# The index and turning chain in steps between the first gate's and the values' products, the second gate's products beside the state space

## The chip, the core and the metric

The kernel runs on one core of one Trainium2 chip. The metric is the device time of one execution in microseconds (us): lower is better. An execution counts from its start to its end on the core. The engines go by the profile's names: PE (TensorE, matrix products), DVE (VectorE), ACT (ScalarE), POOL (GpSimd), and SP, the queue that issues the loads.

## What is computed

Two blocks of two layers each work on x of 256 positions x 1024 channels. The change touches the layers of the first block alone. Cut to what matters, one such layer is:

```python
h = rms_norm(x, norm1_g[l]) * (1.0 + sc1) + sh1
proj = h @ w_in[l]
q, k, v, iq, ik, iw, z, xbc, dt_raw, ga, gm = jnp.split(proj, SPLIT_POINTS, axis=-1)
q = apply_rope(rms_norm(q..., q_norm_g[l]), cos, sin)      # 16 heads of 64
k = apply_rope(rms_norm(k..., k_norm_g[l]), cos, sin)
iq = apply_rope(iq..., cos, sin)                           # 8 index heads of 64
ik = apply_rope(ik..., cos, sin)
# index score of query t for key s <= t: sum_h iw[t,h] * relu(iq[t,h] . ik[s])
# each query keeps its 64 best keys; softmax attention over those
o_attn = dsa_attention(q, k, v, iq, ik, iw, n_keep) @ w_attn_o[l]
xbc = silu(causal_dwconv(xbc, ...));  xs, bm, cm = split(xbc)
y = ssd_scan(xs * dt, a_dt, bm, cm) + xs * d_skip          # state space, 4 groups of 8 heads
y = rms_norm(y * silu(z), ssm_norm_g[l])
o_ssm = y @ w_ssm_o[l]
mixed = (sigmoid(ga) * o_attn + sigmoid(gm) * o_ssm) @ w_out[l]
x = x + g1 * mixed                                         # then a feed-forward part
```

sh1, sc1, g1 and their like come from a small product with `w_ada` ("ada" below). The second block (latent attention, gated linear attention, a diagonal state space and a feed-forward part) is the same in both kernels.

## The kernel before

**Weights.** All weights stream from memory as 639 tiles of 128 x 1024 numbers (512 KB). `weight_plan` lists them in the order in which the products take them, and `make` (line 437) brings one tile: SP loads it into one of five buffers `raw` (line 442), ACT copies it to `whi` (line 445), the part that a product in reduced precision can take, and DVE subtracts that to get the rest, `wlo` (line 446). This pair of steps is called a split. A product of one 128x128 block takes three matmuls: `lin_t` (lines 481 to 483) makes channels x positions, `lin_n` (lines 498 to 500) positions x channels with 512 columns. A tile holds eight blocks, so one product of `lin_t` over all 1024 input channels uses one tile. Splits are made three tiles ahead of their use. The "ada" tiles (`in_ada`, 96 of them) share the five `raw` buffers and are turned by PE at lines 696 and 700, in `ada_part`; `mixed` spreads them between the weight tiles of a part of the plan.

**Order.** Every engine works through its own list, in order. A framework sets the lists ahead of the run, by the order of the program text; loads and splits get a higher priority there. A queue that waits lets nothing behind it pass.

**A layer of the first block** (`block1`, line 822) goes through these parts:

1. The products for dt, index keys and index weights (one narrow tile), for index queries iq, q and k (`lin_n`), with the evictions `evict`, and a short chain for dt.
2. The chain. Index keys `ikd` and index queries `iqr` are rotated by `rope_n` (lines 753 to 767, six DVE operations a call) and turned by PE transposes (`transpose_to`, line 671, copied out by ACT at line 672). Then, for the second and the first half of the queries, PE computes index scores (line 923), ACT takes their relu, DVE adds them up (line 928), and eight rounds of MAX and MATCH_REPLACE (lines 933, 934) take out the 64 best keys and leave a `bias`. Then q and k are rotated with gain tables `tbq`, `tbk` that POOL makes from `rows` (line 750), multiplied by their norm (line 951) and turned again (line 671) to qT and kT.
3. The products of the first gate ga and of the second gate gm: eight tiles each (in layer 1 the first four of ga's come before the layer, `EARLY`), each with one tanh on ACT.
4. B and C of the state space: eight tiles, each with a convolution and silu on DVE and ACT (`conv`, `silu2`, lines 963 and 969), and a small product per group (`cbm`).
5. v: two products of `lin_n`, eight tiles in all.
6. Attention (`attention`, first score at line 778) in steps between the 16 products of x.
7. The state space: for each of 16 pairs of heads decay factors `dd` on DVE and ACT, products with them (line 1079), one product of z (eight blocks), and at some pairs one of `w_attn_o` (`attn_out`, table `ATTN_O`); a norm per group (`ssm_norm`, whose `spread` is line 574 and waits for `rr` of `rsqrt`, line 542).
8. The products of `w_ssm_o` with gm, `w_out`, and the feed-forward part.

`load_rows` (line 740) loads a table into `rows`, which has a single buffer; the load for the second block's first layer stands early in SP's queue, in the middle of layer 0 of the first block.

## Time and profile before

| | |
|---|---|
| three runs | 2380.03, 2381.86, 2384.91 us, median 2381.86 us |
| the profiled execution's own time | 2376.68 us |
| its span | 2374.9 us |
| PE busy | 2225.7 us (94%) |
| PE weight loads busy | 2080.9 us (88%) |
| DVE busy | 1752.4 us (74%) |
| ACT busy | 1324.0 us (56%) |
| POOL busy | 63.0 us (3%) |
| chain that ended last | PE 84%, DVE 11%, DMA 3%, ACT 1%, issue 1% |

The span covers the core's instructions, and the profiled execution's own time is 1.8 us more. A busy share is the sum of the durations over the span; PE's matmuls overlap in the records, so that their starts lie closer than their durations. The chain that ended last is followed back from the last instruction, at each step to what released it. The granted clock (PEclk) is 1.00 for 2.4 GHz and 0.50 for 1.2 GHz; a value between is a mean over a stretch. A row of windows gives the busy times in the order PE, PE's weight loads, DVE, ACT, POOL, each with its instructions (x), then the granted clock, the share of the DMA engines and GB/s. A row of the timeline gives start and length, and in brackets the idle time before it and what ended that.

### The profile page before, as it was taken

What the parts mean: (1) busy time and instruction counts of PE and PEld (TensorE: products, weight loads), DVE (VectorE), ACT (ScalarE), POOL (GpSimd) and SP (SyncE); (2) the same over time, 40 slices, a digit from 0 to 9 for tenths busy, and PEclk for the clock granted to TensorE, in tenths of its full rate; (3) what the DMA queues carried; (4) which work ended last, traced back from release to release, by engine and by line L of the source; (5) the groups of instructions that cost most, each with busy time, mean ns of one, the idle gap of its engine ahead of it and who ended that gap; (6) DMA issues with size and microseconds to landing.
All of it is one profiled execution on the core that took longest, in us unless ns stands there. A gap on an engine that the chain in (4) does not pass through costs nothing.

```text
span 2374.9 us, 46399 instructions
## 1 busy us (share of the span) xinstructions
PE 2225.7 (94%) x18142; PEld 2080.9 (88%) x18142; DVE 1752.4 (74%) x3612; ACT 1324.0 (56%) x2462; POOL 63.0 (3%) x94
## 2 busy tenths in 40 slices
PE   7959998999999969998998999999999999899999
PEld 5848887898998868887898999898999998899999
DVE  4685778858978585788869978867886568668853
ACT  4535666546656534566457655656565456565643
POOL 0000001100000000001100000010000000000000
PEclk8979998999999988999999999999999999999999
DMA  8627443475667526443365566544555547445553
GB/s 292 205 93 253 162 160 125 159 259 170 221 223 254 198 78 229 164 168 134 134 231 162 197 215 208 192 159 140 175 178 183 182 152 224 144 136 176 185 184 125
DMA packets 143466, 429.22 MB, mean 181 GB/s; under 512 B 34864, under 2 KB 40976, under 8 KB 143248
## 3 DMA queue, kind: packets, MB, share of 16 engines
q1 hardware_dynamic: 136496, 422.24, 52.9%
q10 hardware_dynamic: 6752, 4.02, 0.5%
q8 instruction: 143, 2.34, 0.4%
q14 instruction: 75, 0.61, 0.1%
HBM read 413.98 MB, written 12.22 MB: 179 GB/s over the span
## 4 chain that ended last, share of the span: by engine, by line
PE 84%; DVE 11%; DMA 3%; issue 1%; ACT 1%; SPq 0%; ACTq 0%; DVEq 0%
PE pmm L481 21%; PE pmm L482 21%; PE pmm L483 21%; PE pmm L498 3%; PE px L696 3%; PE pmm L500 3%; PE pmm L499 3%; DVE wlo L446 2%; PE px L778 1%; DMA raw<-in_ada 1%; PE px L806 1%; PE px L1079 1%; PE px L700 1%; DVE nv L635 1%; PE px L574 1%
## 5 line engine op out<-in xcount | busy, mean ns | idle before, releaser
L446 DVE TENSOR_TENSOR wlo<-raw,whi 128x1024 fp32r<-128x1024 f32 x639 | 780.4, 1222 | 368.6 <-PE pmm L483 236.9
L445 ACT ACTIVATE whi<-raw 128x1024 fp32r<-128x1024 f32 x639 | 674.6, 1059 | 580.2 <-PE pmm L482 377.6
L481 PE MATMUL pmm<-hh,whi 128*128 128x256 f32 x2464 | 707.9, 288 | 17.6 <-DVE gqk L1520 6.9
L483 PE MATMUL pmm<-hh,wlo 128*128 128x256 f32 x2464 | 704.8, 287 | 2.4 <-DVE wlo L446 2.4
L482 PE MATMUL pmm<-hl,whi 128*128 128x256 f32 x2464 | 705.2, 287 | 0.7 <-DVE hl L525 0.4
L481 PEld LDWEIGHTS pmm<-hh,whi 128*128 128x128 f32 x2464 | 477.3, 194 | 27.9 <-DVE gqk L1520 7.3
L483 PEld LDWEIGHTS pmm<-hh,wlo 128*128 128x128 f32 x2464 | 476.9, 194 | 7.9 <-issue 4.4
L482 PEld LDWEIGHTS pmm<-hl,whi 128*128 128x128 f32 x2464 | 477.6, 194 | 5.3 <-issue 2.8
L481 PE MATMUL pmm<-fh,whi 128*128 128x256 f32 x864 | 244.9, 284 | 0.0
L482 PE MATMUL pmm<-fl,whi 128*128 128x256 f32 x864 | 244.5, 283 | 0.0
L483 PE MATMUL pmm<-fh,wlo 128*128 128x256 f32 x864 | 244.3, 284 | 0.0
L481 PEld LDWEIGHTS pmm<-fh,whi 128*128 128x128 f32 x864 | 165.7, 192 | 0.5
L482 PEld LDWEIGHTS pmm<-fl,whi 128*128 128x128 f32 x864 | 165.8, 192 | 0.2
L483 PEld LDWEIGHTS pmm<-fh,wlo 128*128 128x128 f32 x864 | 165.5, 192 | 0.5 <-issue 0.2
L499 PE MATMUL pmm<-wlo,hh 128*128 128x512 f32 x256 | 101.4, 396 | 0.0
L498 PE MATMUL pmm<-whi,hh 128*128 128x512 f32 x256 | 98.4, 403 | 1.1 <-DVE cvb L963 1.1
L500 PE MATMUL pmm<-whi,hl 128*128 128x512 f32 x256 | 98.8, 394 | 0.0
L696 PE MATMUL px<-raw,cwide 128*32 128x128 f32 x1536 | 76.4, 299 | 5.6 <-DMA raw<-in_ada 5.6
L482 PE MATMUL pmm<-yl,whi 128*128 128x256 f32 x256 | 72.9, 287 | 0.1
L483 PE MATMUL pmm<-yh,wlo 128*128 128x256 f32 x256 | 72.1, 286 | 0.0
L481 PE MATMUL pmm<-yh,whi 128*128 128x256 f32 x256 | 72.0, 286 | 0.0
L696 PEld LDWEIGHTS px<-raw,cwide 128*32 128x32 f32 x1536 | 44.3, 116 | 21.9 <-issue 10.9
(553 smaller groups left out, 4250.8 us busy)
## 6 DMA issues: line engine op xcount, KB each, us to landing
raw<-in_w SPq DMA_DIRECT2D x639, 512.0 KB, 3.7
raw<-in_ada SPq DMA_DIRECT2D x96, 512.0 KB, 4.4
csb<-csd SPq DMA_DIRECT2D x16, 512.0 KB, 5.5
phd<-phases SPq DMA_DIRECT2D x8, 512.0 KB, 3.6
phasel<-phd SPq DMA_DIRECT2D x8, 512.0 KB, 4.6
dpd<-dp SPq DMA_DIRECT2D x4, 512.0 KB, 3.3
gl<-gd SPq DMA_DIRECT2D x32, 64.0 KB, 3.3
bl<-in_s5b SPq DMA_DIRECT2D x4, 512.0 KB, 5.5
```

The lines of the kernel that those rows point to most:

```text
L445: S.activation(hi, raw, AF.Copy)
L446: V.tensor_tensor(lo, raw, hi, OP.subtract)
L481: PE.matmul(ps[:m, :n], wh, src.hi(kt), start=q == 0, stop=False)
L482: PE.matmul(ps[:m, :n], wh, src.lo(kt), start=False, stop=False)
L483: PE.matmul(ps[:m, :n], wl, src.hi(kt), start=False, stop=q == len(kts) - 1)
L498: PE.matmul(ps[t][:, :n], src.hi(kt)[:, ts], w[0], start=start, stop=False)
L499: PE.matmul(ps[t][:, :n], src.hi(kt)[:, ts], w[1], start=False, stop=False)
L500: PE.matmul(ps[t][:, :n], src.lo(kt)[:, ts], w[0], start=False, stop=stop)
L574: PE.matmul(ps[:, col + t * 128:col + (t + 1) * 128], r[:, t:t + 1].to_broadcast([128, 128]), ident, start=True, stop=True)
L635: V.scalar_tensor_tensor(v, xt(j), gcol[:, j:j + 1], self.r, OP.mult, OP.mult)
L696: PE.matmul(pa[32 * j:32 * j + 32, :128], cwide[:, i, :], w[:, i * 128:(i + 1) * 128], start=i < 4, stop=i >= 4, skip_group_check=True)
L700: PE.matmul(pa[:, 128:129], part, half4, start=True, stop=True, skip_group_check=True)
```

## The change

- `weight_plan`: the tiles of v now stand behind ga's and ahead of B's and C's. gm's tiles leave this part; each now stands behind every second z tile of the state space. The ada tiles of `ADA_A` (24 in layer 0, 20 in layer 1) are spread over eight weight tiles fewer.
- The chain (part 2) becomes a generator, `turned`, with a yield between steps; `index_scores` is a generator inside it. Each turning (`turn`) is called one step behind the rotation whose result it turns. The second half's scores now come behind the rotation of q's first half, the first half's behind that of q's second half.
- One step is made after each ga product, three after each half of v, one after each product of B or C, and what is left before the attention.
- gm's products, `gate(gm, ...)`, are made in the state space at the even pairs, behind z's product.

The diff, in which "..." stands for the chain's old text (moved into `turned` as it was):

```diff
--- before.py
+++ after.py
@@ -105,24 +105,25 @@
         a = []
         for c in (C_Q + 512, C_K, C_K + 512):
             a += [("w_in", l, kt * 128, c, 512) for kt in range(8)]
-        for c in (C_GA, C_GM):
-            for j in range(EARLY[l] if c == C_GA else 0, 8):
-                a += _slabs_t("w_in", l, c + j * 128, range(8))
+        for j in range(EARLY[l], 8):
+            a += _slabs_t("w_in", l, C_GA + j * 128, range(8))
+        for c in (C_V, C_V + 512):
+            a += [("w_in", l, kt * 128, c, 512) for kt in range(8)]
         for g in range(4):
             a += _slabs_t("w_in", l, C_XBC + 2048 + g * 128, range(8))
             a += _slabs_t("w_in", l, C_XBC + 2560 + g * 128, range(8))
-        for c in (C_V, C_V + 512):
-            a += [("w_in", l, kt * 128, c, 512) for kt in range(8)]
         plan += mixed(a, ada(l, ADA_A[l]))
         a = []
         for j in range(16):
             a += _slabs_t("w_in", l, C_XBC + j * 128, range(8))
         plan += mixed(a, ada(l, ADA_X[l]))
-        outs = iter(range(8))
+        outs, gms = iter(range(8)), iter(range(8))
         for g in range(5):
             for j in range(4):
                 if g < 4:
                     plan += _slabs_t("w_in", l, C_Z + (4 * g + j) * 128, range(8))
+                    if j % 2 == 0:
+                        plan += _slabs_t("w_in", l, C_GM + next(gms) * 128, range(8))
                 for _ in range(ATTN_O[g][j]):
                     plan += _slabs_t("w_attn_o", l, next(outs) * 128, range(8))
         a = []
@@ -894,23 +895,9 @@
         S.dma_start(csd, dtcs[0:32])
 
 
-        ikd = t256("ikd").rearrange("p (t c) -> p t c", t=2)
...
-        for t in (1, 0):
+        bias, TT = {}, {}
+
+        def index_scores(t, iqT, ikT):
             nk = 128 * (t + 1)
             iws = tiny(8, "iws")
             V.tensor_scalar(iws, mN[:, t, 96:104], IDX_SCALE, None, OP.mult)
@@ -928,6 +915,7 @@
                         V.scalar_tensor_tensor(sc, rl[:, i * nk:(i + 1) * nk],
                                                iws[:, 2 * (j + i) + e:2 * (j + i) + e + 1],
                                                cz if j + e + i == 0 else sc, OP.mult, OP.add)
+            yield
             for r in range(8):
                 m8 = tiny(8, "m8")
                 V.max(m8, sc)
@@ -936,22 +924,51 @@
             V.tensor_tensor(sc, sc, cz, OP.min)
             bias[t] = sc
 
-
-        TT = {}
...
+        def turned():
+            ikd = t256("ikd").rearrange("p (t c) -> p t c", t=2)
+            ikT = t256("ikT")
+            iqT = slot(name="iqT")
             for t in range(2):
+                c_, s_ = rcos[:, t, :], rsin[:, t, :]
+                for r in range(2):
+                    rope_n(ikd[:, t:t + 1, r * 64:(r + 1) * 64], mN[:, t:t + 1, 32:96], c_, s_, c_, s_, 1, 32, V)
+            yield
+            turn = lambda: transpose_to(ikT.rearrange("p (t c) -> p t c", t=2), [ikd[:, t, :] for t in range(2)],
+                                        128, 128)
+            for t in range(2):
+                c_, s_ = rcos[:, t, :], rsin[:, t, :]
+                iqr = t512("iqr")
+                rope_n(iqr.rearrange("p (h d) -> p h d", d=64), iqN[:, t, :].rearrange("p (h d) -> p h d", d=64),
+                       c_, s_, c_, s_, 8, 32, V)
+                turn()
+                yield
+                turn = lambda t=t, iqr=iqr: transpose_to(iqT[:, :, t * 128:(t + 1) * 128],
+                                                         [iqr[:, j * 128:(j + 1) * 128] for j in range(4)], 128, 128)
+            rs = {nm: rsqrt(mean_eps(ss[nm], 32, 64), 32) for nm in "qk"}
+            for nm, gofs in (("q", 0), ("k", 64)):
+                tb = gain_tables(rows, gofs, rcos, rsin, 32, "tb" + nm)
+                TT[nm] = [slot(name=nm + "T"), slot(name=nm + "T")]
+                for t in range(2):
+                    r = rs[nm][:, t * 16:(t + 1) * 16]
+                    xr = slot(name=nm + "r").rearrange("p a b -> p (a b)")
+                    x3 = xr.rearrange("p (h d) -> p h d", d=64)
+                    rope_n(x3, qk[nm][t].rearrange("p (h d) -> p h d", d=64), tb[:, 0, t], tb[:, 1, t],
+                           tb[:, 2, t], tb[:, 3, t], 16, 32, V)
+                    V.tensor_tensor(x3, x3, r[:, :, None].to_broadcast([128, 16, 64]), OP.mult)
+                    turn()
+                    yield
+                    yield
+                    if nm == "q":
+                        yield from index_scores(1 - t, iqT, ikT)
+
+                    def turn(nm=nm, t=t, xr=xr):
+                        for q in range(2):
+                            transpose_to(TT[nm][q][:, :, t * 128:(t + 1) * 128],
+                                         [xr[:, (q * 4 + j) * 128:(q * 4 + j + 1) * 128] for j in range(4)], 128, 128)
+            yield
+            turn()
+
+        side = turned()
         qT = lambda hh: TT["q"][hh // 8][64 * (hh % 2):64 * (hh % 2) + 64, (hh // 2) % 4, :]
         kT = lambda hh: TT["k"][hh // 8][64 * (hh % 2):64 * (hh % 2) + 64, (hh // 2) % 4, :]
 
@@ -968,10 +985,19 @@
             S.activation(th, u, AF.Tanh, scale=0.5)
             V.scalar_tensor_tensor(u, th, 1.0, u, OP.add, OP.mult)
 
-        for gs in (ga, gm):
-            for j in range(EARLY[l] if gs is ga else 0, 8):
-                pg = lin_t("w_in", h, range(8))
-                S.activation(gs[j // 4][:, j % 4, :], pg[:, :T], AF.Tanh, scale=0.5)
+        def gate(gs, j):
+            pg = lin_t("w_in", h, range(8))
+            S.activation(gs[j // 4][:, j % 4, :], pg[:, :T], AF.Tanh, scale=0.5)
+
+        for j in range(EARLY[l], 8):
+            gate(ga, j)
+            next(side, None)
+        vN = [slot(name="vn").rearrange("p a b -> p (a b)") for _ in range(2)]
+        for hf in range(2):
+            for t, p_ in enumerate(lin_n("w_in", h, range(8), 512)):
+                S.activation(vN[t][:, hf * 512:(hf + 1) * 512], p_, AF.Copy)
+            for _ in range(3):
+                next(side, None)
 
         cbms = []
         for g in range(4):
@@ -981,6 +1007,7 @@
                 bc[nm] = t256("cv" + nm)
                 conv(ps[:, :T], "c", 16 + 4 * i + g, 4, bc[nm])
                 silu2(bc[nm])
+                next(side, None)
 
             cbm = t384("cbm")
             pc = px()
@@ -990,11 +1017,8 @@
             S.activation(cbm[:, 128:256], pc[:, 128:256], AF.Copy, scale=0.25)
             V.scalar_tensor_tensor(cbm[:, 256:384], pc[:, 256:384], 0.25, C("tri"), OP.mult, OP.mult)
             cbms.append(cbm)
-        vN = [slot(name="vn").rearrange("p a b -> p (a b)") for _ in range(2)]
-        for hf in range(2):
-            for t, p_ in enumerate(lin_n("w_in", h, range(8), 512)):
-                S.activation(vN[t][:, hf * 512:(hf + 1) * 512], p_, AF.Copy)
-
+        for _ in side:
+            pass
         o = new_hl(8, "o")
 
         ys = [None] * 4
@@ -1089,6 +1113,8 @@
                 S.activation(zz, pz[:, :T], AF.Tanh, scale=0.5)
                 V.scalar_tensor_tensor(zz, zz, 1.0, pz[:, :T], OP.add, OP.mult)
                 V.tensor_tensor(xs[:, pair, :], xs[:, pair, :], zz, OP.mult)
+                if pair % 2 == 0:
+                    gate(gm, 2 * g + pair // 2)
                 attn_out(ATTN_O[g][pair])
                 if pair in NORM_AT and g:
                     if pair == NORM_AT[0]:
```

Three places of the order, before and now. Helper lines are one higher in the changed kernel (446 is 447, 671 is 672, 740 is 741), 923 is 910, 933 and 934 are 921 and 922, 951 is 957, 963 is 980, 969 is 986.

PE, layer 0, from the last product of k to the first tile behind the chain, before (`px` and `pmm` are accumulators, `cst` holds the identity, `raw,cwide` and `half,adap` are ada):

```order
L483 MATMUL pmm<-hh,wlo 128x256
L671 MATMUL px<-cst_75,iqr 128x128 x8
L923 MATMUL px<-ikT,iqT 128x256 x8
L923 MATMUL px<-ikT,iqT 128x128 x8
L671 MATMUL px<-cst_75,qr 128x128 x16
L671 MATMUL px<-cst_75,kr 128x128 x13
L696 MATMUL px<-raw,cwide 32x128 x16
L671 MATMUL px<-cst_75,kr 128x128 x3
```

The same engine and layer in the changed kernel, at the second half's scores (line 910) and q's first turning (line 672):

```order
L499 MATMUL pmm<-whi,hh 128x512
L910 MATMUL px<-ikT,iqT 128x256 x2
L500 MATMUL pmm<-wlo,hh 128x512
L501 MATMUL pmm<-whi,hl 128x512
L499 MATMUL pmm<-whi,hh 128x512
L500 MATMUL pmm<-wlo,hh 128x512
L672 MATMUL px<-cst_75,qr 128x128 x6
L697 MATMUL px<-raw,cwide 32x128 x8
L672 MATMUL px<-cst_75,qr 128x128 x2
```

The turnings and scores of the chain stood in a row on PE; now products of v (lines 499 to 501) stand between them.

DVE, layer 1, at B's and C's convolutions. Before, the chain had ended there and splits and convolutions took turns:

```order
L934 MATCH_REPLACE bias<-m_9877,bias 128x128
L935 TENSOR_SCALAR bias<-bias 128x128
L936 TENSOR_TENSOR bias<-bias,cst_76 128x128
L446 TENSOR_TENSOR wlo<-raw,whi 128x1024 x6
L963 SCALAR_TENSOR_TENSOR cvb<-pmm,pp_78,cvb 128x255
L963 SCALAR_TENSOR_TENSOR cvb<-pmm,pp_78,cvb 128x254
L963 SCALAR_TENSOR_TENSOR cvb<-pmm,pp_78,cvb 128x253
L446 TENSOR_TENSOR wlo<-raw,whi 128x1024
```

Now, between two splits (the first and the last row here are instructions 1236 and 1247; the split before is 1231):

```order
L980 SCALAR_TENSOR_TENSOR cvc<-pmm,pp_78,cvc 128x253
L766 TENSOR_TENSOR ru<-kn,tbk 128x512
L767 TENSOR_TENSOR rv<-kn,tbk 128x512
L922 MATCH_REPLACE bias<-m_10156,bias 128x256
L986 SCALAR_TENSOR_TENSOR cvb<-th,cvb 128x256
L986 SCALAR_TENSOR_TENSOR cvc<-th,cvc 128x256
L768 TENSOR_TENSOR kr<-ru,rv 128x16x32
L921 MAX m_10159<-bias 128x8
L957 TENSOR_TENSOR kr<-kr,rr 128x1024
L922 MATCH_REPLACE bias<-m_10159,bias 128x256
L921 MAX m_10162<-bias 128x8
L447 TENSOR_TENSOR wlo<-raw,whi 128x1024
```

Rotations of k and rounds of the choice of keys now stand among the convolutions: 15 instructions between these two splits, 18 between the second of them and the next.

SP's queue, layer 0, around the load of `rows`, before:

```order
L442 DMA raw<-in_w 128x1024
L692 DMA raw<-in_ada 128x1024
L740 DMA rows<-in_rows 128x192
L442 DMA raw<-in_w 128x1024 x2
L692 DMA raw<-in_ada 128x1024
```

Now:

```order
L693 DMA raw<-in_ada 128x1024
L443 DMA raw<-in_w 128x1024
L741 DMA rows<-in_rows 128x192
L693 DMA raw<-in_ada 128x1024
L443 DMA raw<-in_w 128x1024
```

Before, the load of `rows` stood ahead of the weight tile of gm's first product; now it stands ahead of a tile of the third group's B and C, 13 weight tiles further on.

## Rows read from the trace of the kernel before

**Rows 1.** Waits of PE, whole run: us in total, times, longest.

```profile
PE px L671 <- DVE qr L951: 27.2, 4, 8.8
PE px L574 <- DVE rr L542: 24.5, 7, 7.5
PE px L671 <- DVE kr L951: 19.6, 4, 5.6
```

**Rows 2.** Windows: stretch, us, each engine's busy time, PEclk, DMA share, GB/s.

```profile
102.30:258.60 156.30, 130.47 (x1128) 115.63 (x1126) 106.57 (x235) 68.52 (x138) 4.32 (x8) 0.90 0.53 177
127.50:164.50 37.00, 12.65 (x85) 10.58 (x89) 33.10 (x75) 8.65 (x17) 4.32 (x8) 0.60 0.02 3
832.60:975.40 142.80, 118.81 (x960) 104.19 (x958) 100.54 (x230) 61.06 (x120) 5.24 (x8) 0.86 0.49 164
863.80:895.00 31.20, 8.02 (x47) 6.42 (x46) 30.67 (x69) 5.29 (x13) 5.24 (x8) 0.58 0.00 1
895.00:900.00 5.00, 5.00 (x56) 3.37 (x55) 4.26 (x20) 2.15 (x5) 0.00 (x0) 0.50 0.56 189
900.00:905.00 5.00, 5.00 (x52) 3.48 (x52) 2.66 (x8) 2.58 (x8) 0.00 (x0) 0.50 0.78 252
```

**Rows 3.** Timeline of PE in layer 0: start, us, operation, idle before.

```profile
126.85 1.30 PE L671 MATMUL px<-cst,iqr 128*128 128x128 f32 x8 [0.28 <-DVE iqr L767]
128.84 3.99 PE L923 MATMUL px<-ikT,iqT 64*128 64x256 f32 x32 [0.69 <-ACT iqT L672]
141.63 1.94 PE L671 MATMUL px<-cst,qr 128*128 128x128 f32 x8 [8.80 <-DVE qr L951]
```

**Rows 4.** Timeline of PE at products and one ada column behind it.

```profile
172.01 0.28 PE L481 MATMUL pmm<-hh,whi 128*128 128x256 f32 x1
172.13 0.28 PE L482 MATMUL pmm<-hl,whi 128*128 128x256 f32 x1
...
172.97 0.28 PE L700 MATMUL px<-half,adap 128*128 128x1 f32 x2
...
173.75 0.38 PE L483 MATMUL pmm<-hh,wlo 128*128 128x256 f32 x1
```

**Rows 5.** Waits of SP's queue, 120 to 170 us.

```profile
SPq L740 <- POOL tbk L750: 37.3, 1, 37.3
```

**Rows 6.** Timeline of SP's queue, 120 to 170 us.

```profile
123.38 0.33 SPq L692 DMA_DIRECT2D raw<-in_ada  x1
...
164.66 1.18 SPq L442 DMA_DIRECT2D raw<-in_w  x2
```

**Rows 7.** Groups of DVE, 108 to 300 us: busy us, mean ns, idle.

```profile
L446 DVE TENSOR_TENSOR wlo<-raw,whi 128x1024 fp32r<-128x1024 f32 x42 | 51.3, 1222 | 40.1 <-PE pmm L483 17.7 <-ACT whi L445 12.6 <-PE pmm L499 7.9
...
L933 DVE MAX8 m<-bias 128x8 f32<-128x256 f32 x8 | 3.4, 420 | 0.1
L934 DVE MATCH_REPLACE8 bias<-m,bias 128x256 f32<-128x256 f32 x8 | 3.2, 406 | 0.0
...
L951 DVE TENSOR_TENSOR qr<-qr,rr 128x1024 f32<-128x1024 f32 x2 | 2.4, 1210 | 0.0
...
L963 DVE SCALAR_TENSOR_TENSOR cvc<-pmm,pp,cvc 128x253 f32<-128x253 f32 x4 | 1.9, 478 | 0.1
...
L761 DVE TENSOR_TENSOR ru<-kn,tbk 128x512 f32<-128x512 f32 x2 | 1.5, 740 | 0.0
...
L765 DVE TENSOR_TENSOR ru<-kn,tbk 128x512 f32<-128x512 f32 x2 | 1.4, 680 | 0.0
```

**Rows 8.** Windows of the state space, layers 0 and 1.

```profile
346.60:446.00 99.40, 89.07 (x691) 78.17 (x690) 82.47 (x197) 57.42 (x119) 16.96 (x13) 0.93 0.39 129
1061.70:1161.60 99.90, 87.18 (x690) 77.14 (x689) 83.95 (x206) 59.10 (x127) 18.60 (x20) 0.95 0.37 130
```

**Rows 9.** Waits of PE in the state space of layer 0, from 372 us.

```profile
PE px L574 <- DVE rr L542: 7.5, 1, 7.5
```

**Rows 10.** Waits of PE in the state space of layer 1, from 1088 us.

```profile
PE px L574 <- DVE rr L542: 10.6, 2, 7.5
```

More of the change, by code (lines that the diff above doesn't have):

```diff
@@ L894, in block1 @@
         S.dma_start(csd, dtcs[0:32])
-        ikd = t256("ikd").rearrange("p (t c) -> p t c", t=2)
-        ikT = t256("ikT")
-        iqT = slot(name="iqT")
-        for t in range(2):
-            c_, s_ = rcos[:, t, :], rsin[:, t, :]
-            for r in range(2):
-                rope_n(ikd[:, t:t + 1, r * 64:(r + 1) * 64], mN[:, t:t + 1, 32:96], c_, s_, c_, s_, 1, 32, V)
-        transpose_to(ikT.rearrange("p (t c) -> p t c", t=2), [ikd[:, t, :] for t in range(2)], 128, 128)
-        for t in range(2):
-            c_, s_ = rcos[:, t, :], rsin[:, t, :]
-            iqr = t512("iqr")
-            rope_n(iqr.rearrange("p (h d) -> p h d", d=64), iqN[:, t, :].rearrange("p (h d) -> p h d", d=64),
-                   c_, s_, c_, s_, 8, 32, V)
-            transpose_to(iqT[:, :, t * 128:(t + 1) * 128], [iqr[:, j * 128:(j + 1) * 128] for j in range(4)],
-                         128, 128)
-        bias = {}
-        for t in (1, 0):
+        bias, TT = {}, {}
+        def index_scores(t, iqT, ikT):
             nk = 128 * (t + 1)
@@ L937, in block1 @@
             bias[t] = sc
-        TT = {}
-        rs = {nm: rsqrt(mean_eps(ss[nm], 32, 64), 32) for nm in "qk"}
-        for nm, gofs in (("q", 0), ("k", 64)):
-            tb = gain_tables(rows, gofs, rcos, rsin, 32, "tb" + nm)
-            TT[nm] = [slot(name=nm + "T"), slot(name=nm + "T")]
-            for t in range(2):
-                r = rs[nm][:, t * 16:(t + 1) * 16]
-                xr = slot(name=nm + "r").rearrange("p a b -> p (a b)")
-                x3 = xr.rearrange("p (h d) -> p h d", d=64)
-                rope_n(x3, qk[nm][t].rearrange("p (h d) -> p h d", d=64), tb[:, 0, t], tb[:, 1, t],
-                       tb[:, 2, t], tb[:, 3, t], 16, 32, V)
-                V.tensor_tensor(x3, x3, r[:, :, None].to_broadcast([128, 16, 64]), OP.mult)
-                for q in range(2):
-                    transpose_to(TT[nm][q][:, :, t * 128:(t + 1) * 128],
-                                 [xr[:, (q * 4 + j) * 128:(q * 4 + j + 1) * 128] for j in range(4)], 128, 128)
+        def turned():
+            ikd = t256("ikd").rearrange("p (t c) -> p t c", t=2)
+            ikT = t256("ikT")
+            iqT = slot(name="iqT")
+            for t in range(2):
+                c_, s_ = rcos[:, t, :], rsin[:, t, :]
[35 more added lines that the diff above has]
+            turn()
```

## The prediction

> **What bounds the kernel now.** I read the waits of PE first, since PE is busy 94% of the span and heads the chain that ended last. Of its waits for DVE the largest are those of the turnings: 27.2 us for qr and 19.6 for kr, four each, and between them 24.5 for the norms' rr [rows 1]. All eight waits for qr and kr lie in two stretches, one per layer. In layer 0's stretch of 37.0 us PE is busy 12.65 and DVE 33.10; in layer 1's of 31.2 us PE 8.02 and DVE 30.67 [rows 2]. So the chain is DVE's, and PE waits for each of its steps, up to 8.80 us before one turning [rows 3]. DMA stands at 0.02 and 0.00 there [rows 2]: no raw buffer comes free. PE runs at the lower clock level for much of it (mean 0.60 and 0.58), and in layer 1 products go on at 0.50 for ten us behind the hole [rows 2]. The stage around each hole, from k's last product to the first attention score, takes 156.3 and 142.8 us [rows 2].
>
> **The change, part by part.**
>
> *The holes.* In the new order products of ga, v, B and C stand between the chain's steps, so PE has work while DVE rotates. What is won is the hole less PE's own work in it, which moves along. In layer 0 that work is 12.65 us of busy time at a mean clock of 0.60; all of it halved would be 7.6. Group by group: the last iqr turnings 0.65 and 32 of q and k at 1.94 per eight, both halved for the full clock (0.65 and 3.9), the scores 4.0 as they stand [rows 3], one ada column 1.0 (from 172.97 to 0.23 us behind 173.75) [rows 4]: 9.5. Won: 37.0 − 9.5 = 27.5. In layer 1 the same reading makes 5.4 of the 8.02: 25.8, and about 6 more for the products that run at 0.50 behind the hole, ten us certain and some two beyond. Won: 31.8. Together 59.3.
>
> *gm.* Eight products leave each stage and join the state space: 64 blocks of three matmuls 0.12 us apart [rows 4] are 23.0 us of PE, and eight splits on DVE at 1.222 [rows 7] 9.8. ACT moves with them and has 42 us idle in the state space of layer 0 (57.42 of 99.40) [rows 8]. By itself the move is worth nothing: 23.0 off one place and 23.0 on the other, if PE sets both.
>
> *Does PE set the shorter stage?* Layer 0: 156.3 − 27.5 − 23.0 = 105.8 us for PE, against DVE's 106.57 − 9.8 = 96.8 [rows 2, 7]. It fits, if no split comes late. Layer 1: 142.8 − 31.8 − 23.0 = 88.0, against DVE's 100.54 − 9.8 = 90.7. There DVE is the longer by three us even if it never idles. That is where a new wait must appear: PE for wlo, or for cvb and cvc.
>
> *The new waits.* DVE takes its list in order, so a split stands behind whatever the chain put ahead of it. In layer 1 the order shows 15 instructions between two splits: four conv steps at 0.48, six of the rotation at 0.68 to 0.74 or 1.21 for the multiplication by rr, five of MAX and MATCH_REPLACE at 0.42 and 0.41, two of silu near 0.42 [rows 7]; with the split they come to about 8.5 us less their small overlaps, and the next period to about 8.1. A tile gives PE 24 matmuls at 0.12, 2.9 us, with an ada column 3.9. Three tiles are split ahead, so one such period is covered (8.5 against 3 times 2.9 to 3.9) and two in a row are not: 17 against 12 leave some 5 us, and with the three us above I take 9 for layer 1. In layer 0 the chain is spread over 24 products and DVE has 9 us to spare: 4 for turnings that come while DVE is still at qr or kr. Bounds for both layers together: none at all, and one us on each of the 16 tiles of v, B and C per layer, 32.
>
> *Loads.* The load of rows now blocks SP. Before, it waited 37.3 us for POOL's tbk [rows 5], and no raw tile was issued between 123.38 and 164.66 us [rows 6]. tbk's new version needs its buffer, which DVE's last rotation of k frees. In the new order that load stands 13 weight tiles later, near the time at which the rotation ends. Five raw buffers cover some 7.8 us (two tiles of 3.9) of a block. Between nothing and ten us, I take 2. The bytes themselves fit: about 44 tiles of 0.524 MB in 105 us are 220 GB/s; the queue reached 252 from 900 to 905 us, while PE never paused [rows 2].
>
> *The state space.* PE is busy 89.07 of 99.40 and 87.18 of 99.90 us [rows 8], so 10.3 and 12.7 us are idle there. Most of it is one or two waits at the norm's spread for rr: 7.5 and 10.6 [rows 9, 10]. Where 30 product matmuls stood between a norm's first matmuls and its spread, 163 stand now: 133 more at 0.12 are 16 us of cover. On the other side DVE goes from 82.47 to 92.3 us there, and its splits stand ahead of rr's eleven small steps. Between none and all 23.0 of this idle time is filled; I take 5 a layer, 10.
>
> **Sum.** −59.3 + 4 + 9 + 2 − 10 = −54.3. The profiled execution's own time is 2376.7; that gives 2322.4. The median of the three runs is 5.2 above it, so **2327 us** for the median of the changed kernel. Of the 54 us some 44 come from the stages and 10 from the state space.
>
> **Two rules weighed.** What the order shows for DVE, that a split never passes the rotation ahead of it, is the first place where the sum may be too kind. The Trainium skill, "TensorE: Matmul & The Clock Gate", section "Architectural detail: the array is 16× 32×32, not 1× 128×128", says that ScalarE and VectorE take their queues strictly first in, first out; by that rule each of the chain's pieces delays the split behind it, as in rival A.
> The second is the clock. In the holes the long idle times go with a mean clock of 0.60 and 0.58 [rows 2], and in the state space many short ones with 0.93 and 0.95 [rows 8]. The new stages will have short ones. The same page, section "A second HAM failure mode: psum-queue depth-cycling", says that frequent small idle times between groups of matmuls can make the clock swing between its levels; by that rule rival B holds.
>
> **Rivals.**
>
> A. *The splits queue behind the chain.* One us of wait on each of 32 tiles in place of my 13 in all, so 19 more: **2346**. For it: DVE is 91% and more of the shorter stages (96.8 of 105.8; 90.7 of 88.0). Against it: splits are made three tiles ahead, and the periods of 8 us are few.
>
> B. *The clock swings.* If the stages run at the state space's mean of 0.94, their 194 us of PE work (105.8 + 88.0) lose 6%, 12 us: **2339**. Against it: outside the hole layer 0's stage had (0.90 × 156.3 − 0.60 × 37.0) / 119.3 = 0.99 [rows 2].
>
> C. *All of it is filled.* No new waits, and all 23.0 us of the state space: 15 + 13 less, **2299**. For it: DVE has room in layer 0 and the cover of the norms is twice their wait. Against it: layer 1, where DVE is longer than PE.
>
> D. *DVE becomes the bound through both stages.* PE then waits in the v, B and C tiles for the chain's whole time, 33.1 + 30.7 = 63.8 us, with the 2 of the rows load, and nothing is filled in the state space: −59.3 + 63.8 + 2 = +6.5, so **2388**, slower. It decides from a mean wait of 59.3 less 2 over 32 tiles, 1.8 us a tile; at that point the change is worth nothing, 2382. Against it: outside the holes DVE now idles 119.3 − 73.5 = 45.8 us in layer 0's stage and 111.6 − 69.9 = 41.7 in layer 1's [rows 2], time that the chain's 33.1 and 30.7 us can take.
>
> That the change doesn't do what it says is out: the order shows the chain's matmuls among products, and gm's behind z.
>
> **The numbers.** My forecast 0.52, A 0.20, B 0.10, C 0.10, D 0.04, and 0.04 for D at its turning point, no gain. Faster 0.92, same 0.04, slower 0.04; a measurement of this kernel tells about 0.2%, 4.8 us, from no change. The range leaves out D and most of C: it reaches from 2302, my own terms at their lower bounds (waits of 2, the state space's idle time filled to all but a few us), to 2352, A with little of the state space filled (2346 and 6).
>
> **What would show it.** Right: the waits of PE for qr and kr fall from 46.8 to under 10; no stretch of 30 us with PE under half busy and DMA near zero; first attention score of layer 0 about 110 us behind k's last product, of layer 1 about 97; the half clock behind the hole gone; gm's matmuls in the state space, which takes 117 us (99.4 + 23.0 − 5) with less wait for rr. A would show as PE waiting for wlo at v, B and C, some 30 us; B as a granted clock under 0.96 in the stages; the load of rows as one more gap in SP's raw loads of over 10 us; D as stages of 130 us and more. My sum is wrong if the state space grows by over 25 us, or if the stages lose less than 30 us each beyond gm's 23.

## The result and the profile after

The changed kernel takes 2315.93 us (median of four runs, 2314.76 to 2319.71), the kernel before in the same job 2382.2 us (four runs, 2380.03 to 2384.91). The ratio is 0.9728, with a 95% interval of 0.9711 to 0.9745: 2.7% faster. The forecast was 2327, with a range of 2302 to 2352.

The profiled execution takes 2316.91 us by its own time, with a span of 2315.1, against 2376.68 and 2374.9 before: 59.8 less, where the sum said 54.3. The medians lie 66 apart, since the profiled execution of before was 5 below its median and this one 1 above.

The page's first part, engines over the whole run:

```profile
PE 2214.8 (96%) x18142; PEld 2077.9 (90%) x18142; DVE 1745.4 (75%) x3612; ACT 1319.7 (57%) x2462; POOL 64.8 (3%) x94
```

PE's share rises from 94 to 96%; the work is the same, in a shorter span. The chain that ended last is 88% PE and 7% DVE now, 84 and 11 before. PE's waits over the whole run (columns as in [rows 1]):

```profile
PE pmm L482 <- DVE xs L980: 11.4, 4, 2.9
PE px L799 <- DVE sc L792: 9.5, 3, 4.6
PE pmm L482 <- DVE cvb L980: 9.3, 4, 4.9
PE pmm L482 <- DVE gqk L1546: 7.3, 2, 4.1
PE px L575 <- DVE rr L543: 6.4, 4, 2.1
```

The waits for qr (27.2) and kr (19.6) of [rows 1] are gone, and rr's 24.5 has become 6.4, none of it over 2.1. In their place stand waits for xs and cvb: PE wants an accumulator that a convolution on DVE has not read out yet.

By stage, as windows (columns as in [rows 2]): from k's last product to the first attention score, from there to the first product of w_attn_o, and from there to the first of w_ssm_o, layer 0 and then layer 1:

```profile
103.05:217.20 114.15, 111.09 (x997) 98.33 (x995) 99.52 (x234) 60.98 (x126) 5.69 (x8) 0.99 0.64 218
217.20:306.70 89.50, 82.32 (x603) 74.16 (x603) 73.81 (x176) 57.27 (x144) 0.00 (x0) 0.94 0.41 138
306.70:411.60 104.90, 102.07 (x829) 91.86 (x828) 86.23 (x192) 64.53 (x129) 13.33 (x12) 1.00 0.45 146
798.35:903.30 104.95, 96.67 (x843) 85.90 (x841) 92.72 (x226) 54.09 (x110) 7.57 (x8) 0.98 0.60 200
903.30:991.20 87.90, 80.04 (x588) 71.96 (x588) 73.23 (x177) 56.87 (x145) 0.00 (x0) 0.94 0.40 136
991.20:1096.10 104.90, 102.07 (x828) 91.87 (x827) 86.38 (x189) 63.88 (x128) 17.74 (x19) 1.00 0.43 144
```

The first and fourth answer to the stages of [rows 2], the third and sixth to [rows 8]. The second and fifth, attention beside x's products, were before:

```profile
258.60:346.60 88.00, 83.45 (x629) 73.80 (x629) 76.30 (x175) 60.06 (x147) 0.00 (x0) 1.00 0.44 144
975.40:1061.70 86.30, 83.72 (x629) 73.70 (x629) 74.59 (x166) 58.19 (x139) 0.00 (x0) 1.00 0.43 146
```

PE is busy for 111.09 of 114.15 us where the hole of layer 0 was, at a clock of 0.99 (0.90 before). In layer 1 it is busy 96.67 of 104.95 and DVE 92.72. The state space runs at 1.00 with PE busy 102.07 of 104.90. What has become worse is attention beside x: 0.94 for 1.00, and 7.2 us idle in place of 4.6 in layer 0 and 7.9 in place of 2.6 in layer 1.

| | layer 0 | layer 1 |
|---|---|---|
| k's last product to the first attention score | 156.30 to 114.15 | 142.80 to 104.95 |
| to the first product of w_attn_o | 88.00 to 89.50 | 86.30 to 87.90 |
| to the first product of w_ssm_o | 99.40 to 104.90 | 99.90 to 104.90 |

The first two lines together lose 40.65 and 36.25 us, the third gains 5.5 and 5.0. The rest of the span is 6.6 longer, 3.5 of it right behind the state spaces (up to the first product of w_up), the remainder in parts that the change leaves alone. PE's waits in the first stage of layer 0, then of layer 1, then in layer 0's state space; behind them SP's for the load of rows in layer 0's first stage:

```profile
PE pmm L482 <- DVE cvb L980: 2.4, 2, 2.0
PE px L701 <- ACT adap L700: 0.7, 2, 0.4
```

```profile
PE pmm L482 <- DVE cvb L980: 6.9, 2, 4.9
PE px L701 <- ACT adap L700: 0.7, 1, 0.7
PE pmm L482 <- DVE cvc L980: 0.4, 1, 0.4
```

```profile
PE px L1103 <- DVE xdtn L1057: 1.5, 2, 1.0
PE pmm L482 <- ACT gm L990: 1.3, 1, 1.3
```

```profile
SPq L741 <- POOL tbk L751: 3.6, 1, 3.6
```

That load waits 3.6 us where it waited 37.3 [rows 5], and PE waits for no weight there.

### The profile page after: what moved, and what is told of

It reads as the page before. It is cut to its first block, busy times and chain, and to the rows that moved or that the text cites. A ratio compares the mean times of both kernels' runs of the same rounds, so it can differ in the third digit from the quotient of the medians.

```text
span 2315.1 us, 46342 instructions
## 1 busy us (share of the span) xinstructions
PE 2214.8 (96%) x18142; PEld 2077.9 (90%) x18142; DVE 1745.4 (75%) x3612; ACT 1319.7 (57%) x2462; POOL 64.8 (3%) x94
## 4 chain that ended last, share of the span: by engine, by line
PE 88%; DVE 7%; DMA 3%; ACT 2%; issue 1%; SPq 0%; ACTq 0%; DVEq 0%
PE pmm L482 22%; PE pmm L483 22%; PE pmm L484 22%; PE pmm L499 3%; PE pmm L500 3%; PE pmm L501 3%; PE px L697 2%; DVE wlo L447 2%; DMA raw<-in_w 1%; PE px L779 1%; PE px L807 1%; PE px L1103 1%; ACT whi L446 1%; PE px L672 1%; DMA raw<-in_ada 1%
## 5 line engine op out<-in xcount | busy, mean ns | idle before, releaser
L482 PE MATMUL pmm<-hh,whi 128*128 128x256 f32 x2464 | 712.0, 290 | 38.2 <-DVE xs L980 11.4
L482 PEld LDWEIGHTS pmm<-hh,whi 128*128 128x128 f32 x2464 | 482.4, 196 | 47.1 <-issue 11.3
L484 PEld LDWEIGHTS pmm<-hh,wlo 128*128 128x128 f32 x2464 | 482.1, 196 | 6.2 <-issue 2.9
L483 PEld LDWEIGHTS pmm<-hl,whi 128*128 128x128 f32 x2464 | 482.7, 196 | 4.8 <-issue 2.1
L697 PE MATMUL px<-raw,cwide 128*32 128x128 f32 x1536 | 66.5, 287 | 4.3 <-DMA raw<-in_ada 4.0
```

Of the source, the lines that this page charges most:

```text
L482: PE.matmul(ps[:m, :n], wh, src.hi(kt), start=q == 0, stop=False)
L483: PE.matmul(ps[:m, :n], wh, src.lo(kt), start=False, stop=False)
L484: PE.matmul(ps[:m, :n], wl, src.hi(kt), start=False, stop=q == len(kts) - 1)
L697: PE.matmul(pa[32 * j:32 * j + 32, :128], cwide[:, i, :], w[:, i * 128:(i + 1) * 128], start=i < 4, stop=i >= 4, skip_group_check=True)
```

## Experiments

Times are medians, ratios those to the kernel before on the same chip, which took 2378.61 us beside the steps alone, gm's move alone, v's place alone and gm in the last group; 2377.88 beside gm's and v's move together, turning at once, half of gm in layer 1's first stage and the chain through before B and C; and 2378.87 beside the last three.

**The steps without gm's move.** gm's products and tiles go back behind ga's; nothing else differs from the change.

```diff
+        for j in range(8):
+            gate(gm, j)
...
-                if pair % 2 == 0:
-                    gate(gm, 2 * g + pair // 2)
```

> The chain in steps as in the change, v ahead of B and C, but gm's eight products back in their old stage, behind ga's. Theory: the two parts of the change add up. The state space then falls back to its old waits (99.4 and 99.9 us from the first product of w_attn_o to the first of w_ssm_o, waits for rr of 7 us and more, granted clock about 0.94), which cost 12 us a layer; layer 1's stage gains up to 7 us back, since gm's products give DVE time: 2316 + 24 - 7 to 0, so 2333 to 2340. Rival: gm's move is worth nothing by itself (the state space is shorter for another reason): 2316, within 5.

2333.95 us, 0.9809 (0.9794 to 0.9823): 44.7 less than before. The state space of layer 0 is the old one; layer 1's is 4.3 us shorter than it was (windows of both, PE's waits in layer 0):

```profile
324.77:424.32 99.55, 89.24 (x690) 78.33 (x689) 81.76 (x196) 57.39 (x119) 16.50 (x13) 0.93 0.36 126
1021.05:1116.58 95.53, 87.08 (x690) 76.48 (x689) 82.29 (x193) 57.57 (x119) 20.06 (x21) 0.98 0.38 132
```

```profile
PE px L575 <- DVE rr L543: 7.4, 1, 7.4
PE px L1105 <- DVE xdtn L1059: 2.9, 2, 2.2
```

In layer 1 PE waits 5.4 us for rr there, in two waits, where it waited 10.6 [rows 10]: the theory had its old 99.9 us and did not see this. So the steps are worth 44.7 us and gm's move, on top of them, 18 (2333.95 to 2315.93). The two stretches ahead of the state space are 17.4 and 17.2 us longer than in the change, which is what the six gm products take that the change moves out of them (6 x 2.88 = 17.3): layer 1 won nothing by having gm's products there.

**gm's move without the steps.** The kernel before with gm's tiles and products moved as in the change; the chain stays in one piece and v behind B and C.

```diff
-        for gs in (ga, gm):
-            for j in range(EARLY[l] if gs is ga else 0, 8):
-                pg = lin_t("w_in", h, range(8))
+        for j in range(EARLY[l], 8):
+            gate(ga, j)
...
+                if pair % 2 == 0:
+                    gate(gm, 2 * g + pair // 2)
```

> The kernel before with gm's products moved into the state space and nothing else: the chain in one piece, v behind B and C. Theory: the holes of 37 and 31 us stay as they were (waits for qr and kr 47 us), and the state space with gm takes 105 us instead of 99.4 + 17.3, with no wait for rr above 1 us: 2382 - 24 = 2358, from 2354 to 2362. Rival: the state space was shorter only because the stage ahead of it handed it over differently: 2382, within 5.

2373.63 us, 0.9983 (0.9971 to 0.9995): five us, not 24. The state space did what was expected (104.90, as in the change). The time went elsewhere: in layer 0 the two stretches ahead of it should have lost 17.3 us and lost 1.2, in layer 1 they lost 12.6. (The profiled execution took 2378.93 us, 5.3 above this kernel's median, so that a part of the loss read here may be this execution's own.) Windows of this kernel behind the hole and of its state space, its waits of PE for the ada tiles between 100 and 250 us, then windows of the kernel before at the first two of these times:

```profile
165.00:180.00 15.00, 11.04 (x129) 8.27 (x122) 3.88 (x4) 5.52 (x16) 0.00 (x0) 0.89 0.84 299
180.00:200.00 20.00, 18.32 (x148) 16.39 (x147) 7.08 (x10) 8.02 (x19) 0.00 (x0) 0.74 0.58 204
346.00:450.90 104.90, 102.07 (x828) 91.87 (x827) 86.23 (x192) 64.49 (x129) 13.32 (x12) 1.00 0.43 145
```

```profile
PE px L697 <- DMA raw<-in_ada: 3.5, 3, 1.7
PE px L701 <- ACT adap L700: 1.9, 2, 1.0
```

```profile
165.00:180.00 15.00, 14.19 (x175) 11.94 (x163) 9.20 (x25) 7.72 (x20) 0.00 (x0) 0.98 0.91 336
180.00:200.00 20.00, 20.00 (x209) 17.51 (x209) 7.24 (x6) 10.65 (x23) 0.00 (x0) 1.00 0.84 287
```

Before, PE left the hole at nearly full clock and worked without a pause. Without gm's products there it idles 4.0 and 1.7 us in the first two windows, in short waits for ada tiles, and the granted clock falls to 0.74: a clock 0.26 lower for 20 us is at most 5.2 us of work.

**v's move added to that.** The kernel of the last run, with v's tiles and products ahead of B's and C's.

```diff
+        vN = [slot(name="vn").rearrange("p a b -> p (a b)") for _ in range(2)]
...
         cbms = []
...
-        vN = [slot(name="vn").rearrange("p a b -> p (a b)") for _ in range(2)]
```

> gm's products moved into the state space and v's ahead of B and C, as in the change, but the chain in one piece. It differs from the run with gm alone by the place of v. Theory: with gm alone moved the stage of layer 0 lost 13 us, since B and C with their convolutions and the ada columns then followed right behind the hole, where gm's plain products had stood; v's plain products there give it back, and the state space keeps its 12 us a layer: 2374 - 10 = 2364, from 2360 to 2367. Rival: the loss is the loads' and the clock's, which any product behind the hole meets: 2374, within 4.

2364.67 us, 0.9937 (0.9922 to 0.9952), within the theory's range. Behind the hole:

```profile
165.00:180.00 15.00, 12.39 (x145) 10.10 (x143) 5.67 (x8) 7.62 (x19) 0.00 (x0) 1.00 0.90 308
180.00:200.00 20.00, 20.00 (x129) 15.49 (x130) 7.88 (x7) 9.69 (x16) 0.00 (x0) 1.00 0.74 262
```

With v's products in that place the clock is 1.00 and PE is busy throughout from 180 to 200 us. So behind a hole it matters what follows; and gm's move is worth 13 us without the steps, if v's goes with it. The steps (44.7) and these two moves (13.2) add up to 57.9, and the change gives 66.3, or 63.8 when it was run again.

**v's place alone.** The change with v, and its six steps of the chain, behind B and C.

```diff
-        vN = [slot(name="vn").rearrange("p a b -> p (a b)") for _ in range(2)]
...
+        vN = [slot(name="vn").rearrange("p a b -> p (a b)") for _ in range(2)]
...
         for _ in side:
             pass
```

> The change, with v's products (and the three steps behind each half of v) behind B and C again. Theory: the chain's steps then stand among B's and C's products, each of which brings about 4 us of convolution and silu to DVE, so that PE waits longer for accumulators that cvb and cvc hold: 8 us in layer 1 become 15 to 20, 3 us in layer 0 become 8 to 10, while DVE idles in v's: 2328 to 2336. Rival: where v stands is worth nothing, since the list of DVE is the same in sum: 2316, within 5.

2313.02 us, 0.9719 (0.9702 to 0.9735): no different from the change. The theory fell. With no hole left, v's place is worth nothing: waits of 7.8 us in layer 0's stage, in place of 3.1, but 7.2 in layer 1's, in place of 8.2. The theory's 4 us of DVE work per product of B or C was too much: three convolution steps of 0.48 us and a silu of 0.42 are 1.9.

**Turning at once.** The change delays each turning by a step. Here it is made in the step of its rotation.

```diff
-                    turn()
+                    for q in range(2):
+                        transpose_to(TT[nm][q][:, :, t * 128:(t + 1) * 128],
+                                     [xr[:, (q * 4 + j) * 128:(q * 4 + j + 1) * 128] for j in range(4)], 128, 128)
                     yield
                     yield
```

> The change, with each turning made in the step of its own rotation instead of one step later. Theory: the order of PE's list is set by when operands are reckoned to be ready, so that products still stand between a rotation and its turning, and the delay of a step is worth nothing: 2316, within 4, waits for qr and kr under 5 us in all. Rival: the delay is what lets products cover the rotations; without it PE waits for qr and kr again, 2 to 4 us at each of eight turnings: 2332 to 2348.

2333.91 us, 0.9809 (0.9795 to 0.9824): 18 us lost, as the rival had it in sum, though not by eight waits. Layer 0's stage as windows and its largest waits, then layer 1's largest wait:

```profile
104.20:170.00 65.80, 65.10 (x534) 56.17 (x532) 51.38 (x120) 30.04 (x61) 5.78 (x4) 1.00 0.60 207
170.00:200.00 30.00, 21.47 (x192) 18.57 (x192) 24.39 (x60) 11.53 (x26) 1.35 (x4) 0.79 0.54 164
200.00:231.60 31.60, 29.60 (x280) 27.94 (x278) 24.96 (x54) 17.84 (x39) 0.00 (x0) 0.93 0.64 218
```

```profile
PE pmm L482 <- DVE cvb L977: 4.0, 3, 2.0
PE px L672 <- DVE kr L958: 3.0, 1, 3.0
PE pmm L482 <- ACT whi L446: 2.4, 1, 2.4
```

```profile
PE px L672 <- DVE kr L958: 7.2, 1, 7.2
```

Until 170 us nothing is lost. Then k's rotations come, among B and C. In 30 us PE is idle for 8.5, where the change idles 3.1 in the whole stage, and the clock stands at 0.79, which is at most 6.3 us of work. In the change neither stage has a wait for kr: the delay of a step keeps k's turnings out of PE's way.

**All of gm's products in the last group.** The change with two gm products behind each z of group 3.

```diff
-                if pair % 2 == 0:
-                    gate(gm, 2 * g + pair // 2)
+                for j in range(2 if g == 3 else 0):
+                    gate(gm, 2 * pair + j)
```

> The change, with all eight of gm's products in the last group of the state space, two behind each z, instead of spread over the groups. The state space does the same work. Theory: gm's products gain time as cover for the norms of the first groups; 70 products of 0.12 us now stand ahead of the first norm's spread in place of 172 (30 in the kernel before), so a wait for rr of 3 us comes back there, with some time at the lower clock level: 2316 + 3 to 8 a layer, 2322 to 2332. Rival: any more work on PE there gains the same: 2316, within 4.

2327.2 us, 0.9781 (0.9767 to 0.9796): 11 lost, within the theory's range, though its wait of 3 us came back as one of 7.5 in layer 0 and one of 4.4 in layer 1. In layer 0's state space:

```profile
300.65:421.93 121.28, 113.18 (x890) 102.38 (x889) 94.26 (x214) 69.33 (x139) 14.39 (x13) 0.93 0.41 136
```

```profile
PE px L575 <- DVE rr L543: 7.5, 1, 7.5
PE px L1103 <- DVE xdtn L1057: 0.6, 1, 0.6
```

The old wait of 7.5 [rows 9] is back, and the old clock of 0.93 [rows 8]. It is gm's products as cover for the first norm, not more work in general, that the state space wins by.

**Half of gm in layer 1's first stage**, each with a step of the chain, the other four at the first pair of each group.

```diff
+GM_A = (0, 4)
...
+        for j in range(GM_A[l]):
+            gate(gm, j)
+            next(side, None)
```

> The change, with four of gm's eight products of layer 1 back in its first stage, each with a step of the chain; the other four at the first pair of each group of the state space, which leaves 156 products ahead of the first norm's spread. The same work is done. Theory: layer 1's stage waits for DVE (8 us for cvb, cvc and ada), since it is short of PE work beside the chain; 11.5 us more of it take half of that or more away, and the state space stays without a wait for rr: 2308 to 2313. Rival: these waits come from single late convolutions and not from DVE's sum, so they stay: 2316, within 3; or the state space loses its cover again: 2320 to 2326.

2314.55 us, 0.9727 (0.9711 to 0.9743): no different. The waits in layer 1's first stage fell as the theory had it, from 8.2 to 3.8; the state space, at a clock of 0.94 in place of 1.00, lost that again. PE's waits in the stage, then in the state space of layer 1:

```profile
PE pmm L485 <- DVE cvb L983: 3.8, 2, 2.1
```

```profile
PE px L1109 <- DVE xdtn L1063: 3.4, 2, 2.2
PE px L578 <- DVE rr L546: 2.1, 1, 2.1
```

**The chain through before B and C.** Six steps behind each half of v in place of three.

```diff
-            for _ in range(3):
+            for _ in range(6):
                 next(side, None)
```

> The change, with six steps of the chain behind each half of v instead of three, so that the chain is through before B and C. Theory: the sum of DVE's work in the stage decides, not its place; the waits for cvb and cvc (2 and 7 us) go, and about as much comes as waits for turnings among v's products: 2316, within 5. Rival: the rival of the prediction, splits that queue behind the chain: with the chain denser, waits for wlo and for turnings of one us on each of v's tiles and more: 2326 to 2336.

2315.5 us, 0.9731 (0.9716 to 0.9745): no different, as the theory had it. In layer 1's first stage:

```profile
PE px L672 <- DVE kr L957: 4.3, 1, 4.3
PE pmm L482 <- DVE cvb L980: 3.7, 2, 2.2
```

6.9 us of waits for cvb became 3.7, and 4.3 for a turning came: what one order saves, the other takes.

**The waits that are left.** The change again, and two ways to spread attention's 24 steps over x's 16 products.

```diff
-            for _ in range(24 * (n + LAG) // 16 - 24 * (n + LAG - 1) // 16 if n + LAG else 0):
+            for _ in range([1, 1, 1, 1, 1, 1, 1, 1, 1, 1, 1, 1, 1, 1, 1, 1][n]):
                 next(att, None)
```

(In the third run the list holds no step for the first four products and two for each of the others.)

> The changed kernel itself once more, to set the others beside it on one chip: 2316, within 4.

> The change, with one attention step per product of x instead of the old three for every two products; the eight left over follow the last product. Theory: the largest waits that the change has left are two of 2.9 us per layer among x's products, each with some five us at the lower clock level behind it: four products fill the four accumulators while ACT stands at the attention's copies, and their convolutions start together. In the order this happens once per layer with one step a product, and twice now. A gain of 2.9 and some 2.5 us per layer, less what the eight steps cost behind x: 2305 to 2312. Rival: attention's chain of steps takes its time wherever it stands, and what is won among x's products comes back behind them: 2316, within 4.

> The change, with no attention step before the fifth product of x and two per product from there. Theory: in the order there is still one place per layer where four convolutions start together, and two where two or three do, so it gains less than the run with one step a product: 2310 to 2316. Rival: DVE gets time at the start of x to end the chain, and that is what counts: 2303 to 2309.

2315.03 (0.9735, 0.9722 to 0.9748), 2317.5 (0.9753, 0.9732 to 0.9774) and 2311.83 (0.9723, 0.9710 to 0.9736): three times the same within the intervals. The second run's theory fell; the third run lies in its theory's range, but so does the change run again. With one step a product, from the first attention score of layer 0 through its state space (in an execution of 2327.72 us, 10 above that kernel's median):

```profile
PE px L1103 <- DVE xdtn L1057: 3.6, 2, 2.2
PE pmm L482 <- DVE zs L1114: 3.3, 1, 3.3
PE pmm L482 <- DVE xs L980: 2.9, 1, 2.9
PE pmm L482 <- ACT gm L990: 2.6, 2, 1.3
```

One wait of 2.9 for xs went, and one of 3.3 for zs came, in the state space, where the eight steps left over now stand. No kernel tried here is faster than the change by more than the measurement tells.

## Why the prediction was right

The forecast lies 11 us above the measurement. 5.5 of that is the sum (54.3 where the profiles have 59.8), the rest is where the profiled executions stand beside their medians. The mechanism held, but one term of the sum was less than half of what came, and two agreements are in part luck.

**The holes: right in the sum, in part by luck.** The forecast had 59.3 us won and 15 given back as new waits, 44.3 in all. The steps alone gave 44.7. But in that run's profile the stretches up to w_attn_o lost 23.4 and 19.0 us, 42.4 together, with new waits of 2.3 and 4.8; 4.3 more came in layer 1's state space, which this part of the sum did not contain. No run parts what the holes gave from what the new waits took.

**The new waits: right in size, by another path.** Forecast 4 us in layer 0, for turnings that come while DVE is still at qr or kr, and 9 in layer 1, 5 of them for late splits; the stages have 3.1 and 8.2, and none of it is a wait for qr, kr or wlo. It was the other place that the prediction named, cvb and cvc: convolutions of B and C on DVE have yet to read PE's accumulators, and PE waits for one of those. So the two sizes agree by luck. The longest such wait, 4.9 us in layer 1, ended at 867.02 us. DVE's list around it:

```profile
862.73 0.48 DVE L980 SCALAR_TENSOR_TENSOR cvb<-pmm,pp,cvb 128x254 f32<-128x254 f32 x1
864.04 1.22 DVE L447 TENSOR_TENSOR wlo<-raw,whi 128x1024 fp32r<-128x1024 f32 x1 [0.83 <-ACT whi L446]
...
865.57 0.68 DVE L764 TENSOR_TENSOR kr<-ru,rv 128x512 f32<-128x512 f32 x1
...
866.51 0.46 DVE L980 SCALAR_TENSOR_TENSOR cvb<-pmm,pp,cvb 128x253 f32<-128x253 f32 x1
```

Between the last two steps of one convolution stand a split, which itself waited 0.83 us for ACT, and pieces of the chain. So it is DVE's order that holds PE here, as in rival A, but the convolution queues behind the split and the chain, and not the split behind the chain. The prediction's list of the 15 instructions between two splits adds up to 17; they are three convolution steps, five of the rotation, five of the choice of keys and two of silu. The two periods took 8.4 and 7.0 us, where it said 8.5 and 8.1 (splits at 864.04, 872.46 and 879.47 us).

Rival A, splits that queue behind the chain, gave 2346; in the change PE waits 4.1 us at that matmul for wlo in the whole run, 3.7 before. The denser chain, done before B and C, cost nothing either, against rival A's 2326 to 2336 for that run. That DVE sets layer 1's stage was half right: four gm products more there took 4.4 us of waits away, and nothing off the time.

**The stage lengths: a boundary mis-set.** I gave 110 and 97 us to the first attention score; they are 114.15 and 104.95. In the new order 81 and 95 matmuls of x stand ahead of that score, 9.7 and 11.4 us at 0.12, which I had left out. Over both stretches up to w_attn_o, with six of gm's eight products gone from them (34.5 us), the sum says 59.3 - 15 + 34.5 = 78.8 less; measured are 76.9.

**The state space: the term that was mis-sized.** "Between none and all 23.0 of this idle time is filled; I take 5 a layer, 10." With six of gm's products in it, 17.3 us of PE work, the stretch grew by 5.5 and 5.0 (the 117 us that I gave it counted all eight): 11.8 and 12.3 were won, 24.1 in all and above the bound. The mechanism held: the run with gm in the last group brought the wait of 7.5 back. Two things were mis-sized. Idle time fell from 10.3 and 12.7 us to 2.8 and 2.8, so 17.4 of the 23.0 were filled and not 10. And the bound left out the clock: it had only idle time in it, and with the waits gone the granted clock rose from 0.93 and 0.95 to 1.00 as well. PE's busy time came to 102.07 in both layers, where the old 89.07 and 87.18 with 17.3 more would be 106.4 and 104.5: 4.3 and 2.4 us less for the same work. I had counted the clock as a cost for rival B and not as a gain here. Against these 14 us too little stand 6.6 in the rest of the span that the sum had at nothing. 3.5 of them, behind the state space, came again when the change was run a second time (1.3 and 1.9 more than before there); the remainder is within what the untouched part behind the last of them differs by: 1130.7 to 1138.6 us over the profiled executions of these kernels.

**The loads: harmless, as taken.** SP's wait for the table fell from 37.3 to 3.6 us, and the 2 us that I took for it do not show.

**Rival B, the clock that swings: in one place only.** The stages run at 0.99 and 0.98, and the state space rose. But attention beside x fell from 1.00 to 0.94 in both layers, with two waits of up to 2.9 us for xs in each. When the change was run again, layer 0's showed 0.98 and layer 1's 0.96 with the same waits for xs, so that this cost is not fixed. Nor were the idle times of the old state space many short ones, as the rule was weighed: in layer 0 they were one wait of 7.5 us and two of 2.9 in sum. The Trainium skill, "TensorE: Matmul & The Clock Gate", section "A second HAM failure mode: psum-queue depth-cycling", says that frequent small idle times between groups of matmuls can make the clock swing. The window at 0.74 (gm moved alone), behind and among waits of 1 to 2 us, agrees with it; the one at 0.79 (turning at once) held longer waits too, up to 3.0 us; the stages of the change, at 0.99 and 0.98 with waits of 3.1 and 8.2 us in all, do not show it.

**Rivals C and D.** C had all new waits absent and all 23.0 us of idle time won back in the state space: its second half came true in sum (24.1, of which 17.4 is idle time), its first did not. D, DVE as the bound of both stages, needed 1.8 us of wait per tile; there were 11.3 us over 32 tiles, 0.35.

## What to carry to other kernels

In this kernel it paid to cut a serial chain on one engine into steps between another engine's products (44.7 us), and to ask for what each step hands to that engine one step later (18 us in the change: the list of that engine then waits less at its head). Filler work without dependences was worth most where a short chain of tiny steps (a norm) is waited for, and it had to stand ahead of that wait: the same eight products in the last group gave 11 us less. A reordering on a busy engine moves the waits of the others as well: it matters not only when an operand is ready, but also when an accumulator is read out. Parts of a change need not add up: gm's move alone was worth 5 us, 13 with v's products behind the hole, and 18 once the hole was gone.

## What the runs showed of the hardware

Short waits can come with a lower clock that costs about as much again. With gm moved alone PE was idle 4.0 us of 15 and then 1.7 of 20, and the granted clock of these 20 us was 0.74 (at most 5.2 us of work), at times at which the kernel before ran at 1.00; with turning at once it was 0.79 over 30 us, 8.5 of them idle. Against that the state space of the change ran at 1.00 with three waits of 0.5 to 1.3 us. Where the clock falls is not the same in every execution: one and the same stretch of the change (attention beside x in layer 0, 89.5 and 87.4 us) had 0.94 in one and 0.98 in the other.
